# Four order changes in a two-layer fp32 decoder trunk: output weights held back, an up product moved ahead of the last transposes, scalings queued after the last norm, up weights on GpSimd's DMA queue

## The chip, the cores and the metric

The kernel runs on one core of a Trainium2 chip. The metric is the device time of one launch in microseconds, lower is better. A core has a matmul engine (PE, with its weight loads as PEld), VectorE (DVE), ScalarE (ACT), GpSimd (POOL) and SyncE (SP). Each engine has its own instruction queue and works it off in order. DMAs are issued from the queues of SP, POOL or ACT, and all of them move their data through the same 16 DMA engines.

## The reference

Two decoder layers over 1024 positions with a model width of 1024, all in float32. Each layer normalises its input, runs attention heads (latent attention in layer 0, sliding-window attention with sinks in layer 1, four memory cross-attention heads in both), sends the concatenated heads through an output projection, and adds that to the residual. Then comes the MLP with which this change deals (weights of 1024 x 4096 and 4096 x 1024):

```
def squared_relu_mlp(h, w_up, w_down):
    a = jax.nn.relu(h @ w_up)
    return (a * a) @ w_down

x = x + squared_relu_mlp(rmsnorm(x, mlp_norm_g[i]), mlp_w_up[i], mlp_w_down[i])
```

A final RMSNorm ends the trunk.

## The kernel before

**Precision.** A float32 operand is split into a high and a low part (`split`: ACT line 99 rounds the high part, DVE line 100 subtracts it to get the low part). A product is three matmuls: high by high, high by low, low by high.

**Up products.** `mlp` multiplies the normalised rows with the up weights by Strassen's scheme: seven products, numbered 1 to 7, stand for the eight of a 2 x 2 block product. The 4096 columns are cut into 16 units `i` of 256 columns. A unit's products run in the order 1, 2, 6, 5, 7, 3, 4, each of 12 matmuls over 512 columns (lines 1695 to 1697, `up_mm`). Products 1, 6, 7 and 4 of a unit build up in one PSUM tile `psu`, products 2, 5 and 3 in tiles `psv`. After products 1, 6 and 5, `evac` copies the running sum out with ACT (line 1738). Since product 7 adds to the same `psu` that the copy of product 6 reads, PE may start product 7 only when that copy is done. Product 4's result is read by ACT at line 1742 and by DVE at line 1743, and DVE works out the seven hidden blocks that SP's queue writes to DRAM (`write`, line 1733).

**Up weights.** For each unit `load_raw` (line 1614) brings two halves of 512 KB, h0 and h1, in pieces of 1 KB, into a pair of raw tiles. Even units take the pair `mr`, odd units the pair `d0`, `d1`, so a half of unit i can be loaded when the last reader of the same half of unit i-2 is done; for h1 that is the split of product 4's weights. `gain_w` multiplies a unit's raw weights by the norm's gain (line 1587): four ACT instructions per half. `sum_w` (DVE lines 1630 to 1633) forms Strassen's sums, and `prep_w` splits the seven weight operands, up to four products ahead (`LA`).

**Start of the MLP.** The transposed, normalised rows X1 and X2 come column by column from token tile t (0 to 7): a norm (ACT line 1304 and DVE 1305 in layer 0, ACT line 1506 and DVE 1507 in layer 1), eight PE transposes into `psT_m` (lines 1315 and 1516), and copies (ACT lines 1318 and 1522). For the late tiles DVE forms differences (lines 1322 to 1325 and 1526 to 1529), from which `prep_x` splits the operands X5, X6, X7, X3, X4. Products 1 and 2 of the first two units can start on X1 and X2 alone; their weights come through `fill_w`, apart from the raw tiles. `m.late` holds the transposes that stand inside `mlp`: t=7 in layer 0, t=6 and t=7 in layer 1.

**Down products and the next layer's output weights.** `Down` runs 7 products of 16 steps; a step is 12 matmuls (lines 2045 to 2047). Before a step, `load_a` (line 1910) reads a hidden block back, `load_b` (line 1851) loads down weights in pieces of 512 KB, and `prep` splits both. In layer 0 `WoSums` runs beside the down steps: it loads layer 1's output weights (`w_rows`, line 652, POOL's queue), subtracts blocks on DVE, splits them and writes them to DRAM (line 688, POOL's queue). It does four rounds; `at` puts the load of round k at step 2 + 22k, its subtractions 6 to 9 steps later, its writes 10 to 16 steps later.

**What sets the order.** The program is written in the order of the source. A scheduler then orders each engine's instructions by priority (place in the source) and by its own estimate of times, as far as the data allow. `tc.issue_after(x)` adds an order: what is written inside comes after x. Nothing holds the loads of `WoSums` but their buffers, so those of the first round can be issued while the up products still run.

Of the kernel before, what the change touches and what calls it, by code (L numbers as in the profile page):

```python
# [13 lines left out]
AF = mybir.ActivationFunctionType  # L14
# [41 lines left out]
def trunk(  # L56
# [7 lines left out]
    nc = tc.nc  # L64
    x = x[0]
    out = out[0]
# [26 lines left out]
    def f32(ap):  # L93
        return ap.bitcast(F32)

    def split(src, hi, lo, scale=None):

        if scale is None:
            r = nc.scalar.activation(hi, src, AF.Copy)  # L99
            return r, nc.vector.tensor_tensor(lo, src, f32(hi), ALU.subtract)  # L100
        else:
            nc.scalar.activation(hi, src, AF.Copy, scale=scale)
            nc.vector.scalar_tensor_tensor(lo, src, scale, f32(hi), ALU.mult, ALU.subtract)
# [359 lines left out]
    def raw_tile(shape, name):  # L463
        return quad.tile(shape, F32, tag="raw", bufs=2, name=name)
# [155 lines left out]
    class WoHalf:  # L620
# [12 lines left out]
        def load(self, j):  # L633
            layer, half = self.layer, self.half
            raw = self.raw[j] = raw_tile([P, 2, 512], f"wor{layer}_{half}_{j}")
            cs = slice(half * 512, half * 512 + 512)
            nc.sync.dma_start(out=raw, in_=w_o[layer].rearrange("(k p) n -> p k n", p=P)[:, 2 * j : 2 * j + 2, cs])
# [6 lines left out]
    def w_rows(layer, k, cols, dst, q=nc.sync):  # L644

        if layer == 0 or k > 5:
            q.dma_start(out=dst, in_=w_o[layer, k * P : k * P + P, cols])
            return
        a, e = divmod(k, 3)
        for g in range(2):  # L650
            h = 3 * (2 * a + g) + e
            q.dma_start(out=dst[g * 64 : g * 64 + 64], in_=w_o[layer, h * 64 : h * 64 + 64, cols])
# [3 lines left out]
    class WoSums:  # L656
# [3 lines left out]
            self.s, self.his, self.n = s, his, 0  # L660

        def at(self, n, last):
            k, r = divmod(n - 2, 22)
            if not 0 <= k < 4:
                return
            if r == 0:
                self.load(k)
            elif 6 <= r < 10:
                self.sub(r - 6, last)
            elif r in (10, 12, 14, 16):  # L670
                self.put(k, (r - 10) // 2, last)

        def load(self, k):
            for i, (kt, e) in enumerate(((k, 0), (k, 1), (k + 4, 1), (k + 4, 0))):
                w_rows(1, kt, slice(e * 512, e * 512 + 512), self.s[i], nc.gpsimd)

# [430 lines left out]
    for n in range(len(seq) + LB):  # L1107
# [3 lines left out]
        for lag, late in ((LB, True), (LV, False)):  # L1111
            if 0 <= n - lag < len(seq):
                h, unit = seq[n - lag]
# [20 lines left out]
        h, j = divmod(n, NB)  # L1134
# [47 lines left out]
    def k4(ap):  # L1182
        return ap.rearrange("p (k c) -> p k c", k=4)
# [52 lines left out]
    def wo_phase(layer, wq, o, m):  # L1236
# [36 lines left out]
        xa = {}  # L1273
# [4 lines left out]
        def load(p, half):  # L1278
            t = ORD[half][p]
            dst = m.t(f"i{TORD.index(t)}" if half == 0 else f"i{30 + p % 3}")[:, 0, :]  # L1280
            if half == 0:
                xa[t] = dst
            nc.sync.dma_start(out=dst, in_=m.x_src[rows_(t), half * 512 : half * 512 + 512])
            return dst
# [14 lines left out]
        def norm(p, xb):  # L1299
            y = ys[p] = m.t(f"d{3 + p % 2}")  # L1300
            t = TORD[p]
            rst[t].half(1, xb, y[:, 1, :])
            rs = rst.pop(t).get()
            nc.scalar.activation(y[:, 0, :], xa[t], AF.Copy, scale=rs)
            nc.vector.tensor_scalar(y[:, 1, :], xb, rs, None, ALU.mult)

        def xT_(p):
# [22 lines left out]
        for half, w in enumerate((wq, w1)):  # L1330
# [18 lines left out]
            xs = {0: load(0, half), 1: load(1, half)}  # L1349
            oo = {0: osp(0, (0, 1))}  # L1350
            for p in range(NT):
                t = order[p]
# [6 lines left out]
                hold = layer == 0 and half == 0 and p < 2  # L1359
# [34 lines left out]
    def wo_strassen(layer, wo, o, m):  # L1394
# [87 lines left out]
        def ends(t):  # L1482
            return (a1[t], u2[t]) if t < 4 else (c21[t - 4], a5[t - 4])
# [18 lines left out]
        def norm(t):  # L1502
            rs = rst.pop(t).get()
            xs = ends(t)
            y = yt[t] = xs if t < 4 else ys[t]
            nc.scalar.activation(y[0], xs[0], AF.Copy, scale=rs)
            nc.vector.tensor_scalar(y[1], xs[1], rs, None, ALU.mult)

        def xT_(t):
# [22 lines left out]
        for n in range(N - 8):  # L1532
# [23 lines left out]
            p = steps[n][0]  # L1556
# [12 lines left out]
        for j in range(4):  # L1569
            norm(j)  # L1570
        for i, (p, j) in enumerate(((7, 0), (7, 1), (4, 0), (7, 2), (4, 1), (7, 3), (4, 2), (4, 3))):
# [6 lines left out]
            t = {1: 0, 2: 1, 3: 2, 4: 3, 5: 4, 7: 5}.get(i)  # L1578
# [5 lines left out]
    def scale_w(layer, w, k0):  # L1584

        for k in range(w.shape[1]):
            nc.scalar.activation(w[:, k, :], w[:, k, :], AF.Copy, scale=g_mlp[layer][:, k0 + k : k0 + k + 1])  # L1587
# [15 lines left out]
    def mlp(layer, m, early_w=None, early_mm=None):  # L1603
# [3 lines left out]
        wsrc = mlp_w_up[layer].rearrange("(k p) f -> p k f", p=P)  # L1607
        raws, sums = {}, {}

        def load_raw(i):  # L1610
            r = [m.raw() for _ in range(2)] if i % 2 == 0 else [m.t(f"d{j}") for j in range(2)]
            raws[i] = r = [t_.rearrange("p a (b c) -> p (a b) c", c=256) for t_ in r]
            for h in range(2):
                nc.sync.dma_start(out=r[h], in_=wsrc[:, 4 * h : 4 * h + 4, 256 * i : 256 * i + 256])

        ss = []

        def gain_w(i):
            for h in range(2):
                scale_w(layer, raws[i][h], 4 * h)  # L1620
# [37 lines left out]
        def prep_w(i, p):  # L1658
            a = sums[i][p]
            n = hct[0]  # L1660
            hct[0] += 1
            if n < 7:
                hl.append([k4(v) for v in opens[n]()])
            hi, lo = hl[n % 7]
            split(a, hi, lo)
            return hi, lo
# [6 lines left out]
        def prep_x(p, cols=range(4)):  # L1673
            for j in cols:
                c = slice(j * P, (j + 1) * P)
                if layer and (p != 6 and j < 2 or len(cols) == 4):
                    if j % 2:
                        continue
                    c = slice(j * P, (j + 2) * P)
                src = m.t2[j] if p == 6 else xr[{5: 0, 7: 1, 4: 2, 3: 3}[p]][:, :, c]  # L1680
                hi, lo = [v[:, :, c] for v in X[p]]
                split(src, hi, lo)
# [90 lines left out]
        def go(i, p, w):  # L1773
            evac(i, p, up_mm(i, p, w))
# [4 lines left out]
        load_raw(0)  # L1779
        m.late[0]()  # L1780
        go(0, 1, m.fill[0][1])
        m.late[1]()
        go(0, 2, m.fill[0][2])
        if m.last_a:
            with tc.issue_after(m.last_a.ins):
                gain_w(0)
# [7 lines left out]
        ready[(0, 6)] = prep_w(0, 6)  # L1794
        go(1, 2, m.fill[1][2])
        prep_x(5, range(3))
        gain_w(1)
        sum_w(1)
        ready[(1, 6)] = prep_w(1, 6)
        prep_x(5, (3,))  # L1800
        ready[(0, 5)] = prep_w(0, 5)
        X[7] = [m.t("g0", F32R), m.t("g1", F32R)]
        X[3] = [m.t("g2", F32R), m.t("g3", F32R)]
        prep_x(7)
        ready[(1, 5)] = prep_w(1, 5)
        ready[(0, 7)] = prep_w(0, 7)
        X[4] = [m.t("x0", F32R), m.t("x1", F32R)]
        prep_x(3)
        prep_x(4)
        dn = Down(layer, m, early_w, early_mm)  # L1810
        for n, (i, p) in enumerate(seq):
            for q_ in seq[n : n + LA]:
# [17 lines left out]
    class Down:  # L1830
# [91 lines left out]
        def prep(self):  # L1922
            n = self.order[self.nprep]
            self.nprep += 1
            p, k = self.steps[n]
            a = self.araw.pop(n)
            ah, al, bh, bl = self.set_(n)
            split(a, ah, al)
            self.last = split(self.b({1: 0, 5: 0, 6: 0, 4: 0, 7: 1, 2: 2, 3: 2}[p], k), bh, bl)
            self.ops[n] = (k4(ah), k4(al), bh, bl)  # L1930

        def run(self):
# [464 lines left out]
```

## Time and profile before

| | |
|---|---|
| three runs | 2112.84, 2115.67, 2116.59 us (median 2115.67) |
| the profiled execution | 2113.29 us, span 2111.5 us, granted clock 0.999 |
| PE busy | 2069.2 us, 98% of the span |
| DVE, ACT, POOL busy | 71%, 54%, 9% |
| up products, layer 0 and layer 1 | about 540 to 860 us and 1479 to 1802 us |
| packets of SP's queue (q1), POOL's queue (q0) | 264.25 MB and 25.70 MB |

In the tables of stretches each row gives a window in microseconds from the start of the span, its length, and for each engine the busy time with the number of instructions; then the granted PE clock, the share of the 16 DMA engines' time, and GB/s. A row of a timeline gives start, duration, engine, line and operation, and in brackets how long the engine sat idle before it and what released it. A row of the chain of waits gives start, duration, and what the time went to.

### The profile page before, as it was taken

The page shows a single profiled execution, that of the slowest core. Times are in us where ns is not written, and L with a number is a line of the kernel's source. Part 1 is how long each engine was busy: PE and PEld are TensorE (multiplying, and loading weights), DVE is VectorE, ACT ScalarE, POOL GpSimd, SP SyncE. Part 2 cuts the span into 40 slices and gives each one's busy share as a digit, 9 for nine tenths or more (in the row PEclk, how much of TensorE's full clock was granted, in tenths as well). Part 3 has the DMA queues.
Part 4 walks back from the last instruction along what each step waited for, and adds up shares of the span by engine and source line. Part 5 has one row for each costly group of instructions (what it writes and reads, how often), then busy time and mean ns, then how long its engine had stood idle before and what let it go on. Part 6 is the DMA issues. An engine that isn't in the chain of part 4 may idle for free.

```text
span 2111.5 us, 29192 instructions
## 1 busy us (share of the span) xinstructions
PE 2069.2 (98%) x9880; PEld 1697.1 (80%) x9880; DVE 1496.3 (71%) x2876; ACT 1143.5 (54%) x2461; POOL 192.8 (9%) x284
## 2 busy tenths in 40 slices
PE   7999999999999999999999999999999999999998
PEld 6988777788787878788888878778788878888887
DVE  7556588865977766896667543797976775976565
ACT  5445477776744453444445553877845443444452
POOL 0013000000000000011111231631000000000000
PEclk9999999999999999999999999999999999999999
DMA  7203133342344446976653211146344446844342
GB/s 248 67 1 83 41 74 85 104 146 99 107 168 154 143 143 209 330 234 201 213 169 95 75 31 30 41 147 243 120 149 151 162 138 229 318 150 156 116 119 90
DMA packets 181632, 294.47 MB, mean 139 GB/s; under 512 B 18557, under 2 KB 74346, under 8 KB 181482
## 3 DMA queue, kind: packets, MB, share of 16 engines
q1 hardware_dynamic: 171008, 264.25, 39.4%
q0 software_dynamic: 8048, 25.70, 3.5%
q10 hardware_dynamic: 2426, 2.65, 0.4%
q8 instruction: 78, 1.28, 0.3%
q14 instruction: 72, 0.59, 0.1%
HBM read 194.81 MB, written 85.25 MB: 133 GB/s over the span
## 4 chain that ended last, share of the span: by engine, by line
PE 73%; DMA 10%; DVE 9%; ACT 5%; issue 2%; SPq 1%; POOL 0%; DVEq 0%; ACTq 0%; POOLq 0%
PE psy L2045 5%; PE psy L2047 5%; PE psy L2046 5%; PE psz L2046 4%; PE psz L2045 4%; PE psz L2047 4%; DMA d<-in_mlp_w_up_dram 4%; PE pss L959 4%; PE pso L1001 3%; DMA mr<-in_mlp_w_up_dram 3%; PE psu L1695 3%; PE psu L1697 3%; PE psu L1696 3%; PE psf L108 2%; PE psf L110 2%
## 5 line engine op out<-in xcount | busy, mean ns | idle before, releaser
L1587 ACT ACTIVATE mr<-mr,gcol 128x256 f32<-128x256 f32 (+1 forms) x160 | 67.8, 480 | 78.7 <-DMA mr<-in_mlp_w_up_dram 61.4
L1587 ACT ACTIVATE d<-d,gcol 128x256 f32<-128x256 f32 x128 | 57.8, 503 | 84.0 <-DMA d<-in_mlp_w_up_dram 80.4
L2045 PE MATMUL psy<-g 128*128 128x512 f32 x256 | 99.9, 390 | 0.0
L2046 PE MATMUL psy<-g 128*128 128x512 f32 x256 | 99.6, 389 | 0.0
L2047 PE MATMUL psy<-g 128*128 128x512 f32 x256 | 99.3, 389 | 0.0
L99 ACT ACTIVATE g<-i 128x512 fp32r<-128x512 f32 x79 | 49.7, 629 | 85.6 <-PE psz L2046 42.1
L99 ACT ACTIVATE i<-mr 128x512 fp32r<-128x512 f32 x86 | 54.0, 628 | 68.2 <-PE psy L2046 20.6
L100 DVE TENSOR_TENSOR g<-i,g 128x512 fp32r<-128x512 f32 x79 | 57.7, 730 | 39.7 <-ACT g L99 39.6
L980 ACT ACTIVATE p<-pss 128x512 f32<-128x512 f32 x108 | 63.6, 593 | 41.1 <-PE pss L959 40.7
L99 ACT ACTIVATE uh<-i 128x512 fp32r<-128x512 f32 x66 | 41.6, 631 | 79.6 <-PE psy L2046 38.6
L100 DVE TENSOR_TENSOR pl<-p,ph 128x512 fp32r<-128x512 f32 (+1 forms) x96 | 61.6, 652 | 27.0 <-ACT ph L99 26.5
L834 DVE TENSOR_REDUCE m<-psx 128x1 f32<-128x128 f32 (+5 forms) x96 | 70.3, 749 | 11.0 <-PE psx L830 10.8
L2045 PE MATMUL psz<-g 128*128 128x512 f32 x192 | 74.7, 389 | 0.0
L2046 PE MATMUL psz<-g 128*128 128x512 f32 x192 | 74.7, 389 | 0.0
L2047 PE MATMUL psz<-g 128*128 128x512 f32 x192 | 74.7, 389 | 0.0
L100 DVE TENSOR_TENSOR uh<-i,uh 128x512 fp32r<-128x512 f32 x66 | 45.5, 690 | 39.0 <-ACT uh L99 39.0
L100 DVE TENSOR_TENSOR i<-mr,i 128x512 fp32r<-128x512 f32 x78 | 53.7, 688 | 24.0 <-ACT i L99 23.8
L99 ACT ACTIVATE ph<-p 128x512 fp32r<-128x512 f32 (+1 forms) x96 | 56.4, 599 | 1.3
L2047 PEld LDWEIGHTS psy<-g 128*128 128x128 f32 x256 | 48.1, 188 | 10.0
L2045 PEld LDWEIGHTS psy<-g 128*128 128x128 f32 x256 | 48.1, 188 | 9.9
L2046 PEld LDWEIGHTS psy<-g 128*128 128x128 f32 x256 | 48.1, 188 | 9.8
L1920 DVE TENSOR_TENSOR mqf<-mqq,mqf 128x512 f32<-128x512 f32 x64 | 43.0, 688 | 16.9 <-DMA mqq<-in_mlp_w_down_dram 16.7
(743 smaller groups left out, 6958.4 us busy)
## 6 DMA issues: line engine op xcount, KB each, us to landing
i<-hd SPq DMA_DIRECT2D x154, 256.0 KB
hd<-uh SPq DMA_DIRECT2D x76, 256.0 KB
hd<-ul SPq DMA_DIRECT2D x76, 256.0 KB
mr<-in_mlp_w_up_dram SPq DMA_DIRECT2D x36, 512.0 KB
hd<-x SPq DMA_DIRECT2D x72, 256.0 KB
mr<-hd SPq DMA_DIRECT2D x70, 256.0 KB
d<-in_mlp_w_up_dram SPq DMA_DIRECT2D x32, 512.0 KB
mqq<-in_mlp_w_down_dram SPq DMA_DIRECT2D x32, 512.0 KB
```

The source lines that it names most:

```text
L99: r = nc.scalar.activation(hi, src, AF.Copy)
L100: return r, nc.vector.tensor_tensor(lo, src, f32(hi), ALU.subtract)
L834: nc.vector.reduce_max(m8s[h][:, i : i + 1], ps[:, c], axis=AX, negate=True)
L959: return lambda: nc.tensor.matmul(o, a, b, skip_group_check=True, **kw)
L980: nc.scalar.activation(p, ps, AF.Exp, scale=SC)
L1001: mms.append(lambda: nc.tensor.matmul(o, a, b, skip_group_check=True, **kw))
L1587: nc.scalar.activation(w[:, k, :], w[:, k, :], AF.Copy, scale=g_mlp[layer][:, k0 + k : k0 + k + 1])
L1695: nc.tensor.matmul(ps, wh[:, k, :], xh[:, k, :], start=p in (1, 2, 5) and k == 0, stop=False, skip_group_check=True)
L1696: nc.tensor.matmul(ps, wh[:, k, :], xl[:, k, :], start=False, stop=False, skip_group_check=True)
L2045: nc.tensor.matmul(ps, ah[:, j, :], bh, start=p in (1, 5, 2) and k == 0, stop=False, skip_group_check=True)
L2046: nc.tensor.matmul(ps, ah[:, j, :], bl, start=False, stop=False, skip_group_check=True)
L2047: nc.tensor.matmul(ps, al[:, j, :], bh, start=False, stop=k == NP - 1, skip_group_check=True)
```

## The change

1. `WoSums.at` counts from step 6 with a period of 20 instead of step 2 with a period of 22, and a round's eight loads are written behind a POOL copy of one column. That copy reads the low part of the newest prepared hidden block, so it waits until DVE has made it, and it writes the first target tile. The down step that calls it is step 6 in the first round.
2. `go(0, 2)`, product 2 of unit 0, is written ahead of `m.late[1]()`, the transposes of t=7.
3. `gain_w(1)`, `prep_x(7)`, `prep_x(3)` and `prep_x(4)` are ordered behind the ACT half of the last norm (`m.last_n`).
4. `load_raw` issues the loads of units 2 to 15 on POOL's queue instead of SP's, 28 loads in each layer.

```diff
-            k, r = divmod(n - 2, 22)
+            k, r = divmod(n - 6, 20)
...
             if r == 0:
-                self.load(k)
+                self.load(k, last)
...
-        def load(self, k):
+        def load(self, k, last):
+            hold = nc.gpsimd.tensor_copy(self.s[0][:, 0:1], last[2][:, 0, 0:1])
+            with tc.issue_after(hold.ins):
+                self.load_rows(k)
+
+        def load_rows(self, k):
             for i, (kt, e) in enumerate(((k, 0), (k, 1), (k + 4, 1), (k + 4, 0))):
                 w_rows(1, kt, slice(e * 512, e * 512 + 512), self.s[i], nc.gpsimd)
...
-            nc.scalar.activation(y[:, 0, :], xa[t], AF.Copy, scale=rs)
+            m.last_n = nc.scalar.activation(y[:, 0, :], xa[t], AF.Copy, scale=rs)
...
-            nc.scalar.activation(y[0], xs[0], AF.Copy, scale=rs)
+            m.last_n = nc.scalar.activation(y[0], xs[0], AF.Copy, scale=rs)
...
-                nc.sync.dma_start(out=r[h], in_=wsrc[:, 4 * h : 4 * h + 4, 256 * i : 256 * i + 256])
+                (nc.gpsimd if i > 1 else nc.sync).dma_start(out=r[h], in_=wsrc[:, 4 * h : 4 * h + 4, 256 * i : 256 * i + 256])
...
         go(0, 1, m.fill[0][1])
+        go(0, 2, m.fill[0][2])
         m.late[1]()
-        go(0, 2, m.fill[0][2])
...
-        gain_w(1)
+        with tc.issue_after(m.last_n.ins):
+            gain_w(1)
...
-        prep_x(7)
+        with tc.issue_after(m.last_n.ins):
+            prep_x(7)
...
-        prep_x(3)
-        prep_x(4)
+        with tc.issue_after(m.last_n.ins):
+            prep_x(3)
+            prep_x(4)
...
-            self.last = split(self.b({1: 0, 5: 0, 6: 0, 4: 0, 7: 1, 2: 2, 3: 2}[p], k), bh, bl)
+            self.last = [*split(self.b({1: 0, 5: 0, 6: 0, 4: 0, 7: 1, 2: 2, 3: 2}[p], k), bh, bl), k4(f32(al))]
```

Line numbers of the changed kernel are five higher from `WoSums` on (line 1304 becomes 1309, 1587 becomes 1592), and eight higher behind `mlp`.

**ACT at the start of layer 0's MLP.** The first rows are of the kernel before, the second of the changed one, from the same place: `psT_m_6` and `psT_m_5` are the transposes of t=6 and t=5, line 1304 (1309) with `i_0_4` is the norm of t=6, with `i_0_8` that of t=7, `d_0_87` and `d_0_88` are unit 1's raw weights, `g_0_95` and `g_0_97` parts of X7.

```order
L99 ACTIVATE g_0_95_5807<-x_0_66_5527 128x4x128
L99 ACTIVATE mqf_0_78_5664<-i_0_72_5597 128x4x128
L1587 ACTIVATE d_0_87_5739<-d_0_87_5739,gcol 128x256 x4
L99 ACTIVATE g_0_95_5807<-x_0_66_5527 128x4x128
L1304 ACTIVATE d_0_71_5575<-i_0_4_4844,cosb 128x512
L99 ACTIVATE g_0_97_5809<-x_0_67_5534 128x4x128
L1587 ACTIVATE d_0_88_5740<-d_0_88_5740,gcol 128x256
L1224 ACTIVATE d_0_73_5630,cosb<-i_0_62_5476 128x512
L1318 ACTIVATE x_0_66_5527<-psT_m_6_0_5640 128x4x128
```

```order
L99 ACTIVATE mqf_0_78_5664<-i_0_72_5597 128x4x128
L1309 ACTIVATE d_0_71_5575<-i_0_4_4844,cosb 128x512
L1323 ACTIVATE x_0_66_5527<-psT_m_6_0_5640 128x4x128
L1229 ACTIVATE d_0_73_5630,cosb<-i_0_62_5476 128x512
L1323 ACTIVATE x_0_67_5534<-psT_m_6_1_5646 128x4x128
L1234 ACTIVATE cosb<-cosb 128x1
L99 ACTIVATE mqf_0_79_5665<-x_0_44_5257 128x4x128
L99 ACTIVATE mqf_0_78_5664<-i_0_74_5652 128x4x128
L99 ACTIVATE i_0_101_5823<-mr_80_5666 128x512
L1309 ACTIVATE d_0_73_5630<-i_0_8_4880,cosb 128x512
```

Unit 1's scalings and the splits of X7 have left this place; they come behind the norm of t=7. On PE, product 2 of unit 0 (`psv_0_2`, 12 matmuls) now stands directly behind product 1 of unit 0, ahead of the transposes of t=7; before, four matmuls of unit 1's product 1 stood there. In layer 1 PE has 18 matmuls instead of 4 between the transposes of t=6 and of t=7.

**ACT in unit 5 of layer 0.** `d_0_121` is h1 of unit 5's raw weights, `psu_5` the sum of unit 5's products, which line 1738 (1743) copies after product 1 to `i_0_77` and after product 6 to `d_0_75`; `x_0_105` is a split weight operand.

```order
L99 ACTIVATE i_0_99_5819<-mr_118_6440 128x512
L1738 ACTIVATE i_0_77_5663<-psu_5_6463 128x512
L99 ACTIVATE i_0_101_5823<-mr_119_6441 128x512
L1587 ACTIVATE d_0_121_6580<-d_0_121_6580,gcol 128x256 x2
L99 ACTIVATE x_0_105_5871<-i_0_85_5727 128x512
L1738 ACTIVATE d_0_75_5661<-psu_5_6463 128x512
L1587 ACTIVATE d_0_121_6580<-d_0_121_6580,gcol 128x256 x2
```

```order
L1743 ACTIVATE i_0_77_5663<-psu_5_6463 128x512
L99 ACTIVATE i_0_101_5823<-mr_119_6441 128x512
L1592 ACTIVATE d_0_121_6580<-d_0_121_6580,gcol 128x256 x4
L99 ACTIVATE x_0_105_5871<-i_0_85_5727 128x512
L1743 ACTIVATE d_0_75_5661<-psu_5_6463 128x512
L99 ACTIVATE x_0_105_5871<-i_0_84_5726 128x512
```

Two scalings have moved from behind the copy of `psu_5` to ahead of it. Most other units show the same.

**POOL at the end of layer 0's up products.** `mr_162` and `d_0_159` are the tiles of the first output weights, the last `xd` row is a residual write from before the MLP.

```order
L1382 DMA xd<-i_0_55_5400 128x512
L1382 DMA xd<-i_0_62_5476 128x512
L652 DMA mr_162_8000<-in_w_o_dram 64x512 x4
L652 DMA d_0_159_7997<-in_w_o_dram 64x512 x4
L688 DMA wt5h<-i_0_160_7998 128x512
```

```order
L1619 DMA d_0_136_7691<-in_mlp_w_up_dram 128x4x256
L1619 DMA d_0_137_7692<-in_mlp_w_up_dram 128x4x256
L674 COPY d_0_159_7997<-uh_170_8033 128x1
L652 DMA d_0_159_7997<-in_w_o_dram 64x512 x4
L652 DMA mr_162_8000<-in_w_o_dram 64x512 x4
L693 DMA wt5h<-i_0_160_7998 128x512
```

28 loads of up weights now stand between the last `xd` write and the output weights, and the output weights stand behind the copy of line 674.

## The prediction

> **What bounds the kernel now.** The page's busy times come first.
>
> ```profile
> PE 2069.2 (98%) x9880; PEld 1697.1 (80%) x9880; DVE 1496.3 (71%) x2876; ACT 1143.5 (54%) x2461; POOL 192.8 (9%) x284
> ```
>
> PE is busy for 2069.2 of 2111.5 us, so all its waits together are 42 us, and the change leaves the matmuls as they are. It can win only those waits that lie in its stretches. The tables of stretches for the MLPs of layer 0 and layer 1:
>
> ```profile
> 520.00:540.00 20.00, 17.69 (x89) 14.45 (x88) 17.35 (x42) 15.53 (x36) 1.63 (x3) 1.00 0.33 107
> 540.00:560.00 20.00, 19.86 (x92) 16.26 (x91) 20.00 (x38) 15.74 (x32) 0.00 (x0) 1.00 0.15 53
> 560.00:580.00 20.00, 19.53 (x87) 15.87 (x86) 17.95 (x30) 13.98 (x30) 0.00 (x0) 1.00 0.44 147
> 580.00:840.00 260.00, 256.62 (x1118) 208.74 (x1118) 186.65 (x296) 120.38 (x243) 2.09 (x4) 1.00 0.48 160
> 840.00:860.00 20.00, 16.92 (x74) 13.35 (x72) 9.64 (x16) 6.19 (x11) 2.05 (x4) 1.00 1.01 345
> 860.00:880.00 20.00, 19.82 (x87) 16.45 (x88) 17.47 (x30) 10.03 (x18) 0.00 (x0) 1.00 0.97 352
> 880.00:1120.00 240.00, 240.00 (x1060) 198.79 (x1059) 180.78 (x287) 112.41 (x198) 37.73 (x65) 1.00 0.64 205
> ...
> 1480.00:1500.00 20.00, 17.76 (x85) 14.11 (x85) 20.00 (x43) 19.17 (x36) 1.08 (x2) 1.00 0.10 40
> 1500.00:1520.00 20.00, 19.58 (x85) 15.43 (x84) 17.96 (x25) 14.92 (x28) 0.00 (x0) 1.00 0.45 134
> 1520.00:1780.00 260.00, 257.66 (x1126) 210.33 (x1125) 190.43 (x302) 126.66 (x257) 0.00 (x0) 1.00 0.49 160
> 1780.00:1800.00 20.00, 19.76 (x87) 16.06 (x86) 10.63 (x18) 7.94 (x14) 0.00 (x0) 1.00 0.98 352
> 1800.00:1820.00 20.00, 18.97 (x84) 15.34 (x84) 17.45 (x30) 9.08 (x16) 0.00 (x0) 1.00 0.99 355
> ```
>
> The second number is PE's busy time. Its idle time is 2.31 + 0.14 + 0.47 = 2.9 us at layer 0's start, 3.08 + 0.18 = 3.3 where down begins, then nothing for 240 us; in layer 1 it is 2.24 + 0.42 = 2.7 at the start and 0.24 + 1.03 = 1.3 at down. The row from 880 gives the pace of an unhindered matmul, 240 / 1060 = 0.2264 us, so a unit's 84 matmuls take 19.0. By that pace the two runs of units lose 260 - 1118 x 0.2264 = 6.9 and 260 - 1126 x 0.2264 = 5.1 us; that is more than their idle time (3.4 and 2.3), since the matmuls behind a wait start slowly, and I count by the pace. In all 22.2 us, 1% of the run, are the most that can be had. The clock column is 1.00 throughout.
>
> **Start of the up stage, layer 0.** Timelines of ACT, then PE:
>
> ```profile
> 534.76 1.71 ACT L1587 ACTIVATE d<-d,gcol 128x256 f32<-128x256 f32 x4 [0.83 <-DMA d<-in_mlp_w_up_dram]
> ...
> 536.90 0.71 ACT L1304 ACTIVATE d<-i,cosb 128x512 f32<-128x512 f32 x1
> ...
> 538.03 0.49 ACT L1587 ACTIVATE d<-d,gcol 128x256 f32<-128x256 f32 x1
> ...
> 539.04 1.06 ACT L1318 ACTIVATE x<-psT_m 128x512 f32<-128x512 f32 x2
> ```
>
> ```profile
> 537.66 1.09 PE L1315 MATMUL psT_m<-ident,d 128*128 128x128 f32 x8 [1.39 <-ACT d L1304]
> 539.67 0.50 PE L1695 MATMUL psu<-mqq,uh 128*128 128x512 f32 x1 [0.92 <-ACT x L1318]
> ```
>
> ACT sits 0.83 us waiting for unit 1's weights, then scales them for 1.71, and only then normalises the tile that PE needs; later a scaling and a split delay the copies. Both PE waits, 1.39 + 0.92 = 2.3, go when the scalings and the splits of X7 stand behind the last norm. What is late next is DVE: it has no free time from 540 to 560 (20.00 of 20), and it forms the differences and low parts that product 6 needs. PE would arrive there 2.3 earlier; DVE can follow only as far as its 20 - 17.35 = 2.65 idle before 540 is used. I keep half of the 2.3, and the 0.5 in 560 to 580, where unit 2's product 2 is now put ahead of the product that waits: 1.7, ends 0 and 2.9.
>
> **Start of the up stage, layer 1.** One row of ACT, one of PE, and one of DVE for the price of an operation on 512 columns:
>
> ```profile
> 1490.03 0.71 ACT L1506 ACTIVATE i<-i,sinb 128x512 f32<-128x512 f32 x1
> ```
>
> ```profile
> 1490.80 1.09 PE L1516 MATMUL psT_m<-ident,i 128*128 128x128 f32 x8 [2.24 <-ACT i L1506]
> ```
>
> ```profile
> 661.00 0.68 DVE L100 TENSOR_TENSOR d<-mr,d 128x512 fp32r<-128x512 f32 x1
> ```
>
> With 18 instead of 4 matmuls ahead of these transposes PE has 14 x 0.226 = 3.2 us more to do, so the wait of 2.24 goes. But the same matmuls are then missing behind the transposes, where they covered DVE's six operations (four differences, a split's low part and one operation queued between) from the last copies to X6. There remain 13 matmuls, 2.9 us, against 6 x 0.68 = 4.1 on a DVE that is busy 20.00 of 20. So about 1.2 comes back as a new wait ahead of product 6. I take a gain of 1.2, ends 0 and 2.7.
>
> **Where down begins, layer 0.** Rows of POOL, of the chain of waits, and of PE:
>
> ```profile
> 841.11 2.05 POOL L652 DMA_DIRECT2D d<-in_w_o_dram  x4 [20.64 <-issue]
> ```
>
> ```profile
> 844.19 9.23 DMA mqf<-in_mlp_w_down_dram
> ```
>
> ```profile
> 852.97 0.50 PE L1695 MATMUL psu<-x,d 128*128 128x512 f32 x1 [2.25 <-DVE x L1751]
> ```
>
> Four output-weight loads of POOL meet the first down loads at a DMA share of 1.01; one down load takes 9.23 us, ACT and DVE wait for it, and a copy queued behind on DVE holds PE for 2.25. Layer 1 has the same place without output weights: 1.3 us idle instead of 3.3. With the loads held until step 6 layer 0 should come out like layer 1: a gain of 2.0, ends 0.5 and 2.2. Held loads fall into 860 to 880, where the DMA share is still 0.97. Their cover is the stretch from 880: the output weights of the later rounds are loaded there and PE has no idle time at all. The wait of the hold copy blocks only POOL's own output-weight writes.
>
> **The run of units.** This is the largest term. The chain of waits for one unit, and two rows of SP:
>
> ```profile
> 642.67 4.50 DMA d<-in_mlp_w_up_dram
> ...
> 647.25 0.91 ACT d L1587 x2
> 648.16 0.52 ACT x L99
> 648.68 0.49 ACT d L1738
> ...
> 649.21 0.50 PE psu L1695
> ...
> 658.97 0.91 ACT mr L1587 x2
> ...
> 662.73 4.01 DMA mr<-in_mlp_w_up_dram
> ```
>
> ```profile
> 654.45 0.38 SPq L1614 DMA_DIRECT2D mr<-in_mlp_w_up_dram  x1
> ...
> 658.99 3.65 SPq L1733 DMA_DIRECT2D hd<-uh  x3
> ```
>
> PE's product 7 waits for a copy that ACT does behind scalings of h1. The loads make a closed loop: h1 lands at 647.17; its unit's scalings and sums let h0's load go at 654.45; it is scaled from 658.97 (4.52 later); the h1 tile is free at 661.68, when DVE's split at 661.00 ends; SP reaches h1's load only at 662.73, behind three writes (1.05 late); it lands at 666.74. The turn is 19.57 us against PE's 19.02: 0.55 per unit, and for the 12 units from 4 on in each layer 24 x 0.55 = 13, about the 12 that the pace gave. The loop, not PE, sets this stage's time.
>
> The change does three things to this loop. POOL has nothing else to do there (2.09 us busy in 260), so the 1.05 behind writes goes. Two more scalings, 0.9 us, now stand ahead of the copy, so it ends 2.9 instead of 2.0 after h1 has landed; but the sums behind them start earlier, and I take -0.2 for the turn. Third, both loads get POOL's landing time instead of 4.0 to 4.5. No row shows a 512 KB load in 1 KB pieces on POOL. The nearest rows of the DMA issues:
>
> ```profile
> xd<-d POOLq DMA_DIRECT2D x4, 256.0 KB, 2.3
> ...
> posb<-in_positions_dram POOLq DMA_DIRECT2D x1, 512.0 KB, 4.3
> ```
>
> 256 KB land in 2.3; another 256 KB at the 352 GB/s of 860 to 880 add 0.73, so 3.0; the 512 KB of the positions took 4.3 at the crowded start. I take 3.0 to 4.0. At 4.0 the turn is 19.57 - 0.5 - 1.05 - 0.2 = 17.8; even at 4.3 on both it is 18.4, below PE's 19.0. So PE sets the pace, and the 12.0 go but for waits on something else: I take 9.0, ends 0 and 12 for landings up to about 4.6, and a loss beyond (first rival).
>
> The table shows POOL's DMA instructions from 880 on, 37.73 / 65 = 0.58 us each beside a DVE that is busy for 180.78 of 240: they are not held up. The Trainium skill, "SBUF — State Buffer", section "A bandwidth-pool intuition that's wrong (but worth ruling out)", speaks against the change: beside a DVE copy in its two-port mode a POOL-issued DMA of 620 ns took 3100 ns, since POOL could not write its descriptors. My estimate by that is 2.5 us more on both loads, a turn of 18.3 + 5.0 = 23.3 and a time some 85 us longer; the row of 0.58 disagrees, and DVE's rows here are two-input operations, not copies.
>
> **The sum.** 1.7 + 1.2 + 2.0 + 9.0 = 13.9 us off the profiled execution's 2113.3, so 2099.4. That execution lies 2.4 below the median 2115.7, so the median becomes 2101.8. About 0.2%, 4.2 us, is what a measurement of this kernel can tell from no change: its three runs span 3.75 us.
>
> **The rivals.** *POOL's loads land late* (slower). The loop has two of them per turn, so each us of landing beyond SP's adds two. With landings equal to SP's the turn is 19.57 - 1.05 - 0.2 = 18.3; it meets PE's 19.02 at 0.35 later on each and today's 19.57 at 0.6. At 1.0 later, 5.0 to 5.5, it is 20.3, 0.75 above today: 24 x 0.75 = 18, less the other 4.9, so 2129. It decides from about 0.75 on. For it: a load has four times the descriptors of any POOL row here, if each piece of 1 KB is one, and even 128 KB of output weights take 5.0. Against it: issue costs 2.05 / 4 = 0.51 for 64 rows and 0.54 for 128, so it hardly grows, and those 5.0 were four loads at once in a crowded stretch.
>
> ```profile
> 537.54 0.54 POOL L1382 DMA_DIRECT2D xd<-i  x1 [5.77 <-DVE i L1380]
> ...
> mr<-in_w_o_dram POOLq DMA_DIRECT2D x8, 128.0 KB, 5.0
> ```
>
> Chance 0.13.
>
> *The loop stays*: landings 0.5 to 0.7 later, as by one DVE operation of 0.68 per load if DVE held POOL up, eat what the queue gave. Only 4.9 is left: 2110.8. Chance 0.13.
>
> *Another wait takes over*: ACT's two scalings ahead of the copy and a full DVE at the starts leave half of the unit waits and all of the start waits: 2.0 + 5 = 7 us, 2108.7. Chance 0.14. *The changes cancel*, late loads in some units, gains elsewhere: 2114, chance 0.10.
>
> **How the numbers follow.** The forecast, a loop below PE's pace, has 0.50: 2101.8, own range 2096 to 2107; its low end takes all upper ends, 2.9 + 2.7 + 2.2 + 12.0 = 19.8. The range reaches up over the stayed loop and the cancelled case, 2096 to 2116, and leaves out the slower rival. Some 0.2%, 4.2 us, is what a measurement of this kernel can tell from no change (its three runs span 3.75). Faster, below 2111.4: 0.50 + 0.14 + half of the stayed loop, 0.70. Same: 0.17. Slower: 0.13.
>
> **What would show it.** Right: up-weight loads on POOL landing in 3 to 4 us; in 580 to 840 hardly a PE wait on the copy (line 1743), and about 1148 matmuls at the pace of 0.2264; PE idle from 840 to 880 near 1.3; a small new wait ahead of product 6 in both layers. Wrong: loads of 5 us and more on POOL, ACT's waits for them longer than before, or product 7 still waiting in each unit.

## The result, and the profile after

The changed kernel takes 2148.31 us, the median of five runs (2147.70 to 2150.61). The kernel before takes 2116.59 beside it, also of five (2112.84 to 2117.23). The ratio is 1.0157 with an interval of 1.0146 to 1.0169: the change makes the kernel 31.7 us slower, where a gain of 13.9 was forecast. The profiled execution of after took 2147.70 us, with a span of 2146.0.

The table of stretches shows in one step where the time went. The columns are those of before: PE's busy time and matmuls come second.

```profile
580.00:840.00 260.00, 241.03 (x1038) 193.00 (x1039) 175.89 (x280) 113.06 (x231) 17.98 (x24) 1.00 0.44 144
840.00:860.00 20.00, 20.00 (x90) 16.57 (x89) 11.73 (x18) 6.88 (x12) 0.00 (x0) 1.00 0.65 222
860.00:880.00 20.00, 18.53 (x81) 14.68 (x80) 12.65 (x21) 7.99 (x15) 0.00 (x0) 1.00 0.98 346
1520.00:1780.00 260.00, 244.40 (x1058) 196.73 (x1057) 183.37 (x288) 129.04 (x261) 21.02 (x28) 1.00 0.44 146
```

In the 260 us of layer 0's run of units PE now gets 1038 matmuls done instead of 1118, in layer 1's 1058 instead of 1126. At 0.2264 us each these are 18.1 and 15.4 us, together 33.5 of the 34.5 us between the two profiled spans: the loss lies in the two runs of units. Put as time per unit of 84 matmuls, 260 / 1038 x 84 is 21.0 us and 260 / 1058 x 84 is 20.6, against 19.5 and 19.4 before. The clock stayed at 1.00. Where down begins in layer 0, the loss of 3.3 shrank to 1.5: that edit did what was forecast.

PE's waits in 580 to 840 (total us, times, longest), of before and then of after:

```profile
PE psu L1695 <- ACT d L1738: 2.3, 4, 1.1
PE psu L1695 <- ACT i L1738: 0.9, 4, 0.3
```

```profile
PE psu L1700 <- ACT d L1743: 12.7, 10, 2.0
PE psu L1700 <- ACT i L1743: 6.2, 5, 1.6
```

It is the same wait on ACT's copy: 3.2 us have become 18.9. Most of it, 15.5 us in eleven units, stands ahead of product 7; the rest, in four of them, stands ahead of product 6, which adds to the sum that the copy of product 1 reads. One row of that kind:

```profile
625.40 0.50 PE L1700 MATMUL psu<-mqf,x 128*128 128x512 f32 x1 [1.05 <-ACT d L1743]
```

ACT is late because its weights are. The view of the loading line has the issue on POOL (duration in ns, least, median and longest), who waited, and the time to landing:

```profile
L1619 POOL DMA_DIRECT2D mr<-in_mlp_w_up_dram x28: 748/748/780, 550.2 to 1755.6; - x28
L1619 POOL DMA_DIRECT2D d<-in_mlp_w_up_dram x28: 748/748/765, 564.6 to 1776.8; - x28
...
ACT d L1592: 85.4, 22
ACT mr L1592: 80.6, 25
DMA to landing us min/median/max: 4.3/4.9/6.5
```

The same view of before, where the loads were SP's:

```profile
L1614 SPq DMA_DIRECT2D mr<-in_mlp_w_up_dram x32: 368/384/510, 476.9 to 1725.0; - x32
...
ACT d L1587: 80.4, 25
ACT mr L1587: 58.7, 24
```

A load on POOL lands 4.9 us after its issue, at best 4.3; the forecast took 3.0 to 4.0. ACT's mean wait for a load grew from 139.1 / 49 = 2.8 us to 166.0 / 47 = 3.5.

One turn of the loop, in the timelines of ACT, POOL and DVE in order of time:

```profile
629.84 1.71 ACT L1592 ACTIVATE mr<-mr,gcol 128x256 f32<-128x256 f32 x4 [3.98 <-DMA mr<-in_mlp_w_up_dram]
...
636.36 0.68 DVE L100 TENSOR_TENSOR i<-d,i 128x512 fp32r<-128x512 f32 x1
...
637.34 0.75 POOL L1619 DMA_DIRECT2D d<-in_mlp_w_up_dram  x1 [11.58 <-DVE i L100]
...
642.69 0.51 ACT L1592 ACTIVATE d<-d,gcol 128x256 f32<-128x256 f32 x1 [3.87 <-DMA d<-in_mlp_w_up_dram]
...
644.84 0.68 DVE L100 TENSOR_TENSOR d<-d,d 128x512 fp32r<-128x512 f32 x1
645.30 0.62 ACT L99 ACTIVATE i<-mr 128x512 fp32r<-128x512 f32 x1
...
646.07 0.75 POOL L1619 DMA_DIRECT2D d<-in_mlp_w_up_dram  x1 [7.99 <-ACT i L99]
...
651.40 1.71 ACT L1592 ACTIVATE d<-d,gcol 128x256 f32<-128x256 f32 x4 [4.42 <-DMA d<-in_mlp_w_up_dram]
```

h1 is scaled from 629.84; its sums let h0's load go at 637.34 (7.50 later), which is scaled from 642.69 (5.35); the h1 tile is free when DVE's split ends at 645.52 (2.83); the load of h1 goes at 646.07 (0.55; the trace names ACT's split, which ends at 645.92, as what released it) and is scaled from 651.40 (5.33). The turn is 21.56 us, one of the longer ones. The five pieces of this kind serve for all kernels below, from start to start in each one's own rows, and from DVE's end to the second load's start for the fourth. For before, two rows complete those that the prediction shows, the split that releases h0's load and the scaling that ends the turn:

```profile
653.74 0.68 DVE L100 TENSOR_TENSOR i<-mr,i 128x512 fp32r<-128x512 f32 x1
...
666.83 0.91 ACT mr L1587 x2
```

| Piece, us | before | after |
|---|---|---|
| h1 scaled -> load of h0 | 7.20 | 7.50 |
| load of h0 -> scaled | 4.52 | 5.35 |
| -> h1 tile free | 2.71 | 2.83 |
| -> load of h1 | 1.05 | 0.55 |
| load of h1 -> scaled | 4.10 | 5.33 |
| turn | 19.58 | 21.56 |

In this turn landings cost 0.83 + 1.23 = 2.06 more. The queue gave back only 0.50, and lost 0.30 of that again in the first piece, since POOL issues h0's load 0.30 us after the end of the split that releases it (637.04); SP did so 0.03 after it (654.42, then 654.45).

The turns differ, so here are the medians over units 4 to 15 of both layers, 24 loads of each half. The third row is the third and fourth piece together.

| Piece, us, median | before | after |
|---|---|---|
| h1 scaled -> load of h0 | 7.20 | 7.48 |
| load of h0 -> scaled | 4.50 | 5.18 |
| h0 scaled -> load of h1 | 3.76 | 3.38 |
| load of h1 -> scaled | 4.10 | 4.88 |
| turn | 19.57 | 20.98 |

So landings cost 0.68 + 0.78 = 1.46 per turn on the median, and the queue gave back 0.38 - 0.28 = 0.10. The turn grew by 1.41, and 24 times that is 34.

Three theories went into the runs. *A: POOL's loads land late, and the loop adds both up* (the slower rival). *B: the two more scalings that now stand ahead of ACT's copy hold PE.* *C: the held output weights or the edits at the starts cost the time.*

### The profile page after: what moved, and what is told of

It is laid out like the page before. It is cut to its first block, busy times and chain, and to the rows that moved or that the text cites. A ratio compares the mean times of both kernels' runs of the same rounds, so it can differ in the third digit from the quotient of the medians.

```text
span 2146.0 us, 29217 instructions
## 1 busy us (share of the span) xinstructions
PE 2074.5 (97%) x9880; PEld 1694.8 (79%) x9880; DVE 1492.9 (70%) x2876; ACT 1142.4 (53%) x2461; POOL 246.2 (11%) x344
## 5 line engine op out<-in xcount | busy, mean ns | idle before, releaser
L1700 PE MATMUL psu<-g,i 128*128 128x512 f32 x120 | 49.4, 412 | 31.3 <-ACT d L1743 18.4
L1700 PEld LDWEIGHTS psu<-g,i 128*128 128x128 f32 x120 | 22.5, 187 | 44.7 <-ACT d L1743 23.4
L2055 PEld LDWEIGHTS psy<-g 128*128 128x128 f32 x256 | 48.0, 188 | 10.1
```

The costliest lines, as they stand in the source:

```text
L1700: nc.tensor.matmul(ps, wh[:, k, :], xh[:, k, :], start=p in (1, 2, 5) and k == 0, stop=False, skip_group_check=True)
L2055: nc.tensor.matmul(ps, al[:, j, :], bh, start=False, stop=k == NP - 1, skip_group_check=True)
```

## Experiments: which edit costs the time

**Loads back on SP, the other three edits in.**

```
-(nc.gpsimd if i > 1 else nc.sync).dma_start(out=r[h], ...
+nc.sync.dma_start(out=r[h], ...
```

> The changed kernel with the up-weight loads back on SP's queue; the other three edits stay. Theory A (the loads land later from POOL's queue: in the changed kernel 5.3 us from issue to the first scaling, against 4.0 to 4.5 before, twice in each turn of the load loop) expects the turn back at 19.6 us, the whole slowdown gone, and the gain forecast for starts and down, 4.9 us: about 2112. Theory B (the two scalings that now stand ahead of the copy cost the time) expects the same here, as ACT's order in the units is that of before again. Theory C (the hold of the output weights or the new order at the starts costs the time) expects over 2140.

Measured: 2110.92, ratio 0.9981 (0.9972 to 0.9991). With SP's queue the slowdown is gone, and what is left of the change gains 4.0 us.

**Before, with only the loads moved to POOL.**

```
-nc.sync.dma_start(out=r[h], ...
+(nc.gpsimd if i > 1 else nc.sync).dma_start(out=r[h], ...
```

> The kernel before with only the up-weight loads of units 2 to 15 on POOL's queue. Theory A expects the whole slowdown without the small gains elsewhere: 32 + 4.9, so about 2153, with loads landing some 5 us after issue. Theory B expects the same, since ACT's order in the units follows. Theory C expects about 2116.

Measured: 2152.59, ratio 1.0176 (1.0153 to 1.0199), 37 us slower than before. The moved loads alone make the whole loss and 4 us more, the 4 that the first run has the other edits gain. C falls.

**Before, with only the output weights held.**

```
-k, r = divmod(n - 2, 22)
+k, r = divmod(n - 6, 20)
...
+hold = nc.gpsimd.tensor_copy(self.s[0][:, 0:1], last[2][:, 0, 0:1])
+with tc.issue_after(hold.ins):
```

> The kernel before with only the output weights held until step 6. If the down loads of layer 0 were slowed by the output-weight loads, as forecast, the wait of 2.25 us in 840 to 860 goes and the time falls by 2.0: 0.999 of before. If the held loads only move the crowding, no change.

Measured: 2111.88, ratio 0.9985 (0.9976 to 0.9994), so a gain of 3.2 us, between 1.3 and 5.1. The stretches from 840 and a step of the chain of waits:

```profile
840.00:860.00 20.00, 18.98 (x84) 15.29 (x83) 12.90 (x21) 8.39 (x15) 0.00 (x0) 1.00 0.99 355
860.00:880.00 20.00, 20.00 (x90) 16.53 (x90) 17.07 (x28) 9.89 (x17) 4.66 (x9) 1.00 1.04 313
```

```profile
841.33 6.84 DMA mqf<-in_mlp_w_down_dram
```

The down load that took 9.23 takes 6.84. PE's idle time falls from 3.26 to 1.02, and although the held loads now stand in 860 to 880, with a DMA share of 1.04, PE is busy there for all 20.00. The cover that the forecast named holds.

**Before, with only the starts changed** (product 2 of unit 0 ahead of the last transposes, scalings and splits behind the last norm).

```
+go(0, 2, m.fill[0][2])
 m.late[1]()
-go(0, 2, m.fill[0][2])
...
-gain_w(1)
+with tc.issue_after(m.last_n.ins):
+    gain_w(1)
```

> The kernel before with only the two order edits at the starts of the MLPs (product 2 of unit 0 earlier, scalings and splits behind the last norm). From the trace of the changed kernel with loads on SP I expect layer 0's start 1.4 us shorter and layer 1's 1.7 longer, so no change in all, 1.000; the forecast of 1.7 + 1.2 would be 0.9986.

Measured: 2113.32, ratio 0.9995 (0.9986 to 1.0003): no difference that can be told. PE's waits in 525 to 560 and in 1455 to 1530, as this kernel has them:

```profile
PE psu L1697 <- DVE d L100: 1.0, 1, 1.0
PE psu L1695 <- ACT x L1318: 0.2, 1, 0.2
PE psT_m L1315 <- ACT d L1304: 0.2, 1, 0.2
...
PE psu L1695 <- ACT mqf L99: 1.3, 1, 1.3
PE pswy L1472 <- DVE sinb L1232: 1.1, 1, 1.1
PE psT_m L1516 <- ACT i L1506: 0.5, 1, 0.5
PE psu L1696 <- DVE mqf L100: 0.3, 1, 0.3
```

In layer 0 the two waits of 1.39 and 0.92 fall to 0.2 each, and a wait of 1.0 on DVE's split comes up in a later product: 2.3 became 1.4. The wait of 0.5 in 560 to 580 became 0.2. In layer 1 the 2.24 fell to 0.5, but 1.3 and 0.3 stand at product 6. The 1.1 in attention's last output projection does not come from this edit, though before has 0.2 there: the kernel with the hold alone, whose starts are as before, has it too.

```profile
PE pswy L1477 <- DVE sinb L1237: 1.3, 1, 1.3
```

Without that wait layer 1's waits are 2.1, where before has 2.2 and 0.3. The time still did not fall: after the last matmul of that projection PE's next 120 matmuls take 29.9 us here, and 28.4 to 29.4 in the five kernels whose layer 1 starts as before. What layer 0's start wins, layer 1's gives back in part.

## Experiments: the queue, the pieces and the landing

**Loads on SP, all writes to POOL.** This frees SP as the change meant to, without POOL's landing, and it keeps the two more scalings ahead of the copy.

```
-nc.sync.dma_start(out=hd[p][i * P : (i + 1) * P, :], in_=a)
+nc.gpsimd.dma_start(out=hd[p][i * P : (i + 1) * P, :], in_=a)
```

> The changed kernel with the loads on SP and the writes of hidden blocks on POOL's queue instead. ACT has the four scalings of h1 ahead of the copy, as in the changed kernel, but the loads are SP's and no write stands ahead of them. Theory A expects loads landing in 4.0 to 4.5, a turn of 19.6 - 1.05 = 18.5, below PE's 19.02, so the unit waits go: 2116.6 - 4.9 - 9 to 12, so 2100 to 2103. Theory B expects the copy to stay late by the two scalings and PE to wait in each unit as in the changed kernel: 2130 to 2148.

Measured: 2111.84, ratio 0.9992 (0.9979 to 1.0006). The run of units, PE's waits in it, and a row of ACT:

```profile
580.00:840.00 260.00, 258.21 (x1136) 212.67 (x1136) 190.12 (x301) 122.75 (x245) 53.44 (x99) 1.00 0.49 164
```

```profile
PE psu L1700 <- ACT d L1743: 1.2, 2, 0.9
```

```profile
666.77 1.71 ACT L1592 ACTIVATE mr<-mr,gcol 128x256 f32<-128x256 f32 x4 [1.72 <-DMA mr<-in_mlp_w_up_dram]
```

1136 matmuls, and 1.2 us of waiting for the copy are left, all of it before 632 us: B falls, for the four scalings (x4) still stand together ahead of the copy in most units. The run of units is near PE's pace as soon as nothing holds SP. But the time hardly moved. In this kernel a wait of 1.8 on DVE and one of 0.8 stand in down, where there was 1.0, and layer 1's start loses some 3 us more than with the writes on SP; it differs from the first run of this study in the writes' queue alone, so the writes cause it. By which path stays open.

**POOL's loads in pieces of 4 KB.** Each load reads 128 rows of 4 KB instead of 512 pieces of 1 KB, still 512 KB.

```
+nc.gpsimd.dma_start(out=r[h].rearrange("p k c -> p (k c)"),
+    in_=mlp_w_up[layer][P * (i % 8) : P * (i % 8) + P, 1024 * h : 1024 * h + 1024])
```

> The changed kernel with each up-weight load on POOL taking 128 rows of 4 KB instead of 512 pieces of 1 KB, so as many bytes in a quarter of the pieces; it loads other weights than the units need, so the output is another. Theory A with the count of pieces as the cause expects POOL's issue back near 0.55 us, landing in 3.0 to 3.5 and no unit waits: 2100 to 2105. Theory A with the queue itself as the cause (whatever the pieces) expects landings near 5 and about 2148. Theory B expects about 2148 too, but with early landings.

Measured: 2124.36, ratio 1.0048 (1.0036 to 1.0061). Its stretch, its issues (KB each, us to landing), and two rows of a turn:

```profile
580.00:840.00 260.00, 251.64 (x1093) 203.90 (x1092) 183.97 (x292) 118.15 (x239) 12.90 (x24) 1.00 0.45 152
```

```profile
mr<-in_mlp_w_up_dram POOLq DMA_DIRECT2D x28, 512.0 KB, 4.3
d<-in_mlp_w_up_dram POOLq DMA_DIRECT2D x28, 512.0 KB, 4.7
```

```profile
664.72 0.54 POOL L1620 DMA_DIRECT2D mr<-in_mlp_w_up_dram  x1 [7.73 <-ACT i L99]
...
669.02 1.71 ACT L1592 ACTIVATE mr<-mr,gcol 128x256 f32<-128x256 f32 x4 [2.92 <-DMA mr<-in_mlp_w_up_dram]
```

The issue takes 0.54 instead of 0.75, the loads land 0.4 to 0.5 earlier by these medians (the changed kernel has 4.8 and 5.1 there), and in this turn h1's is scaled 4.30 after its issue; the medians are 4.76 for h0 and 4.34 for h1, instead of 5.18 and 4.88. The run of units is at 260 / 1093 x 84 = 20.0 us per unit. By the ratios 0.0109 of the 0.0157 lost go with the pieces and 0.0048 stay. These loads also read other rows of the weights, and the runs do not separate that from the size of the pieces.

**SP's loads in the same pieces**, everything else as in the first run of this study.

```
-nc.gpsimd.dma_start(out=r[h].rearrange("p k c -> p (k c)"), ...
+nc.sync.dma_start(out=r[h].rearrange("p k c -> p (k c)"), ...
```

> The loads on SP with 128 rows of 4 KB instead of 512 pieces of 1 KB, the other three edits in (other weights are loaded, so the output is another). On POOL that shortened issue from 0.75 to 0.54 us and the landing by 0.5 to 1.0. If the count of pieces is a cost of POOL's queue, SP's landing stays at 4.0 to 4.5 and the time at that of the same kernel with 1 KB pieces, about 0.998 of before. If the pieces are a cost of the transfer itself, SP's loads land earlier by about as much, the unit waits go, and the time falls by 5 to 9 us: 0.995.

Measured: 2098.53, ratio 0.9928 (0.9913 to 0.9943). Both runs of units, then four rows of a turn:

```profile
580.00:840.00 260.00, 260.00 (x1147) 214.97 (x1147) 190.31 (x300) 123.45 (x246) 0.00 (x0) 1.00 0.50 167
1520.00:1780.00 260.00, 260.00 (x1148) 215.29 (x1148) 187.54 (x296) 123.90 (x248) 0.00 (x0) 1.00 0.50 168
```

```profile
653.06 0.33 SPq L1620 DMA_DIRECT2D mr<-in_mlp_w_up_dram  x1
...
657.30 0.91 ACT L1592 ACTIVATE mr<-mr,gcol 128x256 f32<-128x256 f32 x2 [2.93 <-DMA mr<-in_mlp_w_up_dram]
...
661.06 0.38 SPq L1620 DMA_DIRECT2D mr<-in_mlp_w_up_dram  x1
...
664.85 0.91 ACT L1592 ACTIVATE mr<-mr,gcol 128x256 f32<-128x256 f32 x2 [2.32 <-DMA mr<-in_mlp_w_up_dram]
```

PE has no idle time at all in either run of units, 1147 and 1148 matmuls, as the forecast said for a loop below PE's pace. Only some 0.3 us less on each landing (4.24 and 3.79 for 4.52 and 4.10; by medians 4.15 and 3.77 for 4.50 and 4.10) did that, with SP's wait behind the writes still in place. So 12 us are to be had in the runs of units, and the landing of the loads decides on them to a few tenths of a microsecond. With equal pieces POOL's loads (medians 4.76 and 4.34) remain 0.6 behind SP's. The time says the same: in 4 KB pieces POOL's loads lose 1.0048 - 0.9928 = 0.0120 against SP's, 25 us, where in 1 KB pieces they lost 0.0176, 37 us. So shorter pieces seem to be a cost on both queues, and some two thirds of the loss stay with POOL's queue.

**After, with the writes of units 2 to 13 on POOL too**, so that SP's queue has none of them beside the loads.

```
-nc.sync.dma_start(out=hd[p][i * P : (i + 1) * P, :], in_=a)
+(nc.gpsimd if 2 <= i < 14 else nc.sync).dma_start(out=hd[p][i * P : (i + 1) * P, :], in_=a)
```

> The changed kernel with the hidden-block writes of units 2 to 13 on POOL's queue too, so loads and writes stand in one queue as before, only POOL's. If a POOL load lands late because SP's writes share the DMA engines with it, landings fall back to about 4.3 to 4.5 us, the turn to about 19.8 us, and the time to 2112 to 2120. If making its descriptors on POOL is what is late, landings stay near 5.3, the wait behind the writes comes on top, and the turn is 21.5 to 22.2: 2150 to 2176.

Measured: 2144.45, ratio 1.0139 (1.0122 to 1.0157). The run of units, the time to landing from the view of the loading line, and a row of ACT:

```profile
580.00:840.00 260.00, 244.45 (x1039) 195.83 (x1040) 174.55 (x280) 112.84 (x232) 63.58 (x108) 0.99 0.44 144
```

```profile
DMA to landing us min/median/max: 4.2/4.6/6.8
```

```profile
671.61 0.91 ACT L1592 ACTIVATE mr<-mr,gcol 128x256 f32<-128x256 f32 x2 [4.46 <-DMA mr<-in_mlp_w_up_dram]
```

The loads land 4.6 us after their issue instead of 4.9; by medians they are scaled 4.93 (h0) and 4.48 (h1) after it, 0.25 and 0.40 sooner than in after. But h1's load now waits for POOL as it did for SP: from h0's scaling to h1's load it is 4.27 us, where after has 3.38. The turn is 21.15, and a unit takes 260 / 1039 x 84 = 21.0 us, as in after: the queue eats the gain. Neither forecast fits as a whole. SP's writes account at most for a part of the late landing, and as the writes still run beside the loads, only from another queue and in another order, the run does not show which part. The last row bears on theory B: only two scalings (x2) stand ahead of the copy here in most units, and the units are as slow as with four.

**Only h0's loads on POOL, and only h1's.**

```
-(nc.gpsimd if i > 1 else nc.sync).dma_start(out=r[h], ...
+(nc.gpsimd if i > 1 and h == 0 else nc.sync).dma_start(out=r[h], ...
```

> The changed kernel with only the first halves (h0) loaded by POOL, the second by SP. By the load loop h0's load costs 0.27 of POOL's answer and 0.83 of landing more per turn, so 20.7 us against 19.57, in some 25 units: 27 us, less the 4 of the other edits: about 2137, 1.011. If instead only the second half's load decides (it is the one ahead of the copy that PE waits for), no loss: 2111.

> The changed kernel with only the second halves (h1) loaded by POOL, the first by SP. By the loop: 1.05 of waiting behind writes goes, 0.55 of POOL's answer and 1.27 of landing come, so 20.35 us against 19.57: 20 us in some 25 units, less 4: about 2130, 1.008. If the two halves share one cause that needs both on POOL, about 2111.

Measured: 2138.35, ratio 1.0105 (1.0091 to 1.0118) for h0, and 2124.21, ratio 1.0037 (1.0023 to 1.0050) for h1. Rows of each:

```profile
660.96 0.75 POOL L1619 DMA_DIRECT2D mr<-in_mlp_w_up_dram  x1 [20.86 <-DVE i L100]
...
666.26 0.51 ACT L1592 ACTIVATE mr<-mr,gcol 128x256 f32<-128x256 f32 x1 [4.62 <-DMA mr<-in_mlp_w_up_dram]
```

```profile
668.10 0.75 POOL L1619 DMA_DIRECT2D mr<-in_mlp_w_up_dram  x1 [19.51 <-DVE d L100]
```

With h0 on POOL its load is scaled 5.30 after its issue, while h1 on SP keeps 1.05 of waiting and lands as before: a turn of 20.65. With h1 on POOL its load goes 0.30 after the split's end and is scaled 5.23 later: 20.24. Over units 4 to 15 of both layers the median turns are 20.64 and 19.84. h0's ratio is as the loop has it; h1's loss is smaller than the 1.008 expected, though the sign holds. Set against the kernel with all loads on SP the two lose 26 and 12 us, together 38, and after, with both, loses 37: the landings add up, as in a closed loop.

## Experiments: a version that beats both

The writes have no reader for a long time, so they are what should leave SP's queue; the run with all writes on POOL lost outside the run of units. So only those of units 2 to 13 go, with the loads on SP: once with the hold and the start edits in layer 0 alone, once with the hold alone.

```
+(nc.gpsimd if 2 <= i < 14 else nc.sync).dma_start(out=hd[p][i * P : (i + 1) * P, :], in_=a)
```

> What the runs so far point to: loads on SP, the writes of units 2 to 13 on POOL's queue (later units' writes on SP, since POOL then has output weights to fetch), the hold, and the start edits in layer 0 alone. Expected: unit waits gone in both layers (3 + 4 us against the changed kernel with loads on SP), layer 1's start as before, down as with SP writes: 6 to 11 us below before, 0.996.

> The kernel before with the hold of the output weights and with the writes of units 2 to 13 on POOL's queue; both starts as before. Beside the mixed version (0.9948), which also has layer 0's start edits: without their 1.4 us I expect 0.9955.

Measured: 2102.20, ratio 0.9948 (0.9935 to 0.9960), and 2105.10, ratio 0.9950 (0.9938 to 0.9963). Both beat before by 11 us and after by some 44 (0.0207 to 0.0209 of 2115). The first one's runs of units:

```profile
580.00:840.00 260.00, 259.17 (x1140) 213.13 (x1139) 188.49 (x298) 122.41 (x244) 45.40 (x84) 1.00 0.49 165
1520.00:1780.00 260.00, 259.18 (x1142) 213.80 (x1142) 187.91 (x297) 123.43 (x246) 45.42 (x84) 1.00 0.49 167
```

260 - 1140 x 0.2264 = 1.9 and 260 - 1142 x 0.2264 = 1.5 us are lost there, of 6.9 and 5.1 before. The intervals of the two overlap, so the start edits in layer 0 alone are not shown to gain.

The medians show that part of what the freed queue wins is lost again in the landing. In the first of the two SP issues h1's load 2.74 us after h0's scaling instead of 3.76, so the wait behind the writes is gone. But that load, now issued beside POOL's writes, is scaled 4.73 after its issue instead of 4.10; h0's takes 4.19 instead of 4.50. That is still enough for a turn of 19.03, PE's pace.

## Why the prediction was wrong

**The step that failed** is the sum for the load loop, in two of its terms. The first is the landing on POOL: "I take 3.0 to 4.0". It is 4.9, and by medians 5.18 (h0) and 4.88 (h1) from issue to first scaling. The estimate went from a 256 KB row to 512 KB by the bandwidth of a full stretch. But that row was a store out of SBUF in rows of 2 KB, and the load is 512 pieces of 1 KB; pieces of 4 KB land in 4.3 to 4.7 on the same queue. The nearer row was the positions' 4.3, put aside as belonging to a crowded start. The prediction's case against the rival, that an issue hardly grows with its rows, held from 64 to 128 rows (0.51, 0.54) but not to 512 pieces (0.75), and told nothing of the landing.

**The second term** is the wait behind the writes, 1.05, which was to vanish. POOL answers 0.55 us after the split's end at h1 and 0.30 at h0, so 0.85 of it came back. The -0.2 for sums that start earlier came out as +0.1 in the turn read. Of a queue gain of 1.25 per turn, 0.08 was left there, and 0.10 by the medians. Both terms were needed for the loss: by the prediction's own sum, the measured landings with the full queue gain make a turn of 18.3 + 1.46 = 19.8, only 0.2 above before, and the time would have come out near no change. The measured turn is 20.98. That is also why the loss passed the slower rival's 2129.

**The loop itself was right**: h0's and h1's landings are in series, PE's pace of 19.0 is the floor, 24 turns count. h0 alone and h1 alone add up to both; a few tenths less on SP bring PE to 260.00 of 260; and 1.4 us more per turn, 24 times, are the 33 or 34 lost. Of the rivals *POOL's loads land late* holds, with the lost queue gain added to it. *Another wait takes over* falls in the units: the writes on POOL leave 1.2 us of copy waits with four scalings ahead of the copy, and with two ahead of it (loads and writes on POOL) the units are as slow as in after. Why a load lands later from POOL's queue stays open.

By the prediction's estimate from the Trainium skill, "SBUF — State Buffer", section "A bandwidth-pool intuition that's wrong (but worth ruling out)", a load beside DVE's copies would land 2.5 us later; here the loads are scaled 0.7 to 0.8 later by the medians, and the issue takes 748 to 780 ns in all of its 56 cases, so no such lock-out shows. The loss that it pointed to came by another way. The Trainium skill, "DMA: Bandwidth & Descriptors", section "Anatomy of one DMA — SWDGE (gpsimd) path", has a fit of 2.0 us plus the bytes at 436 GB/s for a DMA on GpSimd's queue; my estimate by it is 3.2 us for 512 KB, as short as the prediction's. The measured 4.9 decides.

**The held output weights** were right: 2.0 forecast, 3.26 to 1.02 in the stretch, and 3.2 (1.3 to 5.1) by the clock. **Layer 0's start** was right in kind: DVE does follow late, as said, and the waits fell by 0.9 + 0.3 = 1.2 of the forecast 1.7. **Layer 1's start** was wrong in sign: the waits at product 6 came back larger (1.6) than the 1.2 named, and the same 120 matmuls took 29.9 us, not less than the 28.4 to 29.4 without the edit. Together the starts gain 1.1, between -0.6 and 3.0, for a forecast of 2.9. For all three edits 4.9 was forecast and 4.0 measured.

## What to carry to other kernels

Where buffers make a closed loop, the landing time of a load counts as often as loads stand in series in a turn, so measure a moved load's landing in its own shape (queue, direction, pieces) before moving it. To free a queue for urgent loads, move what nobody waits for soon, here the writes, and leave the loads where they land soonest. A wait behind a queue's other work is removed by another queue only as far as that one answers sooner: here 0.85 of 1.05 us came back. And read a loop's pieces over many turns: the one turn read here overstated the landings, 2.06 more where the median was 1.46.

## What the runs showed of the hardware

- A 512 KB load in 1 KB pieces was scaled 4.50 (h0) and 4.10 us (h1) after its issue on SP in the kernel before, and 5.18 and 4.88 on POOL in the changed one; in 4 KB pieces 4.15 and 3.77 on SP, 4.76 and 4.34 on POOL (medians of 24 loads each). With the longer pieces, which also read other rows, both queues' loads came 0.3 to 0.5 sooner.
- A DMA issue occupied POOL for 0.75 us with 512 pieces and 0.54 with 128, SP for about 0.38 and 0.33 to 0.38.
- POOL issued a load 0.30 us after the end of the split that released it (0.55 at h1 in the changed kernel), SP 0.03 after it where nothing stood ahead in its queue.
- How much of POOL's late landing comes from its own queue, and how much from SP's writes beside it, stays open: with the pieces equal 0.6 us remain, and with the writes on POOL's queue too the loads were scaled 0.25 to 0.40 sooner. On SP, h1's load took 0.6 us longer when the writes went by POOL's queue.
